# A hybrid decoder layer: the order of two token norms, the first transfers, and how x is added to three blocks of the output projection

## The chip, the cores and the metric

The kernel runs on one core of one Trainium2 chip (trn2). The metric is the device time of one execution in microseconds (us); less is better. The kernel before took 2128.58 us, the median of three runs (2126.21, 2128.58 and 2132.4).

## What is computed

One decoder layer over 512 tokens of width 2048, with 256 memory tokens. All inputs and the output are float32.

```python
xn = rms_norm(x, attn_norm_g)
gq, gk, gv, gg, ga, fq, fk, fv, fg, ff, mq, mg = split(xn @ w_in)
gla_o = gla_chunked(...)                 # 8 gated-linear-attention heads
fox_o = forgetting_attention(...)        # 4 heads
mem_o = softmax(mq . mk) @ mv            # 4 heads; mk, mv = rms_norm(mem, mem_norm_g) @ w_mem_kv
o = rms_norm(concat(gla_o, fox_o, mem_o), out_norm_g)
h = x + (o * gates) @ w_out
u = relu(rms_norm(h, mlp_norm_g) @ w_up)
y = h + (u * u) @ w_down
```

`rms_norm(v, g)` is `v * rsqrt(mean(v*v) + 1e-6) * g`.

## The kernel before, in words

**Precision.** Every operand of a large product is split in two: a rounded high part, which ScalarE writes (a CAST, L168 or L367; `ahi_x` L186 for x), and the remainder, which VectorE writes from the operand and the high part (a TENSOR_TENSOR, L169 or L367; `alo_x` L187). One product then takes three matmuls, high by high (L176), high by low (L177), low by high (L178), in `mm3`. A weight tile is thus loaded by a DMA from SyncE (SP), cast by ScalarE (ACT), subtracted by VectorE (DVE), and only then multiplied by TensorE (PE).

**Stages.** The program goes through the input projection, the attentions, the output projection (`out_pair`, twice), the up projection (eight groups) and the down projection. The input projection begins with `project("gk", "gq")`, which goes over 16 tiles of x and multiplies each by two groups of columns. After it come four products `in_pair(n, c)`, c outside and n inside. `in_pair` and `out_pair` are written as seven block products, in the order 1, 5, 6, 3, 7, 2, 4 (as in Strassen's scheme, with sums of blocks as operands); a product is two steps in an `in_pair` and four in an `out_pair`, one split weight tile (128x1024) to a step. When a product is complete, `after` empties its two PSUM banks.

**The norm of x.** The input projection multiplies x without its norm; the factor of each token, `xrstd`, is applied when banks are emptied. `x_tile(k)` loads x's tile (`xraw`), splits it and adds its squares to `xacc`. `token_rstd` (L222) then sums `xacc` over the partitions by four small matmuls (`ss_x`, L226) and computes 1/sqrt with a chain of small operations on DVE and ACT (`s_x` L119, `y_x` L120 and L121, `z_x` L122 to L124, `r_x` L125). The banks of the first product of `in_pair(0, 0)` are emptied by ACT with that factor (`o`, L492), so they wait for `r_x`.

**The memory's norm.** Before the pairs the kernel loads 16 tiles of the memory (`memT`, L509), squares them (ACT, `sq_mem`, L219), adds the squares (DVE, into a part of `spare`, L220) and calls `token_rstd` again (`ss_mem`, two small matmuls on PE at L226). The factor is first used in the memory's projections, after the pairs.

**The sums of x.** Four of the seven products of a pair have sums of blocks of x as operands. `x_sums(0)` writes those of c = 0 into `sh` and `sl`. `x_sums(1)` computes those of c = 1 and writes them to DRAM (`x_op`, by DMAs from GpSimd, POOL). While `in_pair(1, 0)` runs (n = 1, c = 0), `next_sums` brings each of the four back when the product that read its place is done: a load on SP (L450), a copy by ACT (L451), a subtraction by DVE (L452).

**The output projection.** Its first pair emits h's left half in blocks (row, column) of 256 tokens by 512 columns. `block(r, c)` loads x's block into a staging tile (L1270, SP), and the products add into it: 1 to (0,0), 5 to (1,1), 6 to (0,1), then 3, 7, 2 and 4. Each bank is added by DVE (L1275). `finish` writes a complete block to DRAM and prepares it for the up projection.

**What sets the order.** A scheduler places instructions on the engines' queues by priority and by when it estimates that operands are ready; `high_priority` moves one forward, and `issue_after` puts one behind another. Each engine works through its queue in order.

Of the kernel before, what the change touches and what calls it, by code (L numbers as in the profile page):

```python
# [9 lines left out]
F32 = mybir.dt.float32  # L10
# [8 lines left out]
NT = S // 128  # L19
# [28 lines left out]
def hybrid_layer(  # L48
# [45 lines left out]

    colt = const.tile([128, 68], F32, name="colt")
    with tc.high_priority(offset=AHEAD):
        nc.sync.dma_start(colt, cols)
    g_attn, g_mem, g_out, g_mlp = (colt[:, 16 * i : 16 * i + 16] for i in range(4))
    g_fq, g_fk, g_mq, g_mk = (colt[:, 64 + i : 65 + i] for i in range(4))

# [93 lines left out]
    def tmp(name, tag, n=512, dt=F32):  # L194
        return tp.tile([128, n], dt, tag=tag, name=name, bufs=TAGS[tag])
# [36 lines left out]
    def project(*groups):  # L232

        banks = [[(abank if i else gbank)(f"{g}_{t}") for t in range(NT)] for i, g in enumerate(groups)]
        for kp in range(NK // 2):
            for ps, group in zip(banks, groups):
                wh, wl = wtile(w_in[GROUPS.index(group), kp], f"{group}{kp}", parts=1 if kp else 2)
                for kk in range(2):
                    k = 2 * kp + kk
                    ah, al = x_tile(k)  # L240
                    for t in range(NT):
                        cs = slice(kk * 512 + t * 128, kk * 512 + t * 128 + 128)
                        mm3(ps[t], wh[:, cs], wl[:, cs], ah, al, k == 0, k == NK - 1)
        return [p for ps in banks for p in ps]
# [159 lines left out]


    kq = project("gk", "gq")
    xrstd = token_rstd(xacc, NT, "x")
    kTs = bigt(0, [128, NT, 512], "kTs")
    qTs = bigt(1, [128, NT, 512], "qTs")
    with urgent():  # L410
# [36 lines left out]

    def next_sums(n):
        hi, lo = sh[:, n, :, :], sl[n // 2][:, n % 2, :, :]
        nc.sync.dma_start(lo.bitcast(F32), x_op[n])  # L450
        A.copy(hi, lo.bitcast(F32))  # L451
        V.tensor_sub(lo, lo.bitcast(F32), hi.bitcast(F32))  # L452


    places = [[(1, 1), (1, 2)], [(0, 0), (0, 1)], [(0, 2), (1, 0)]]
# [1 line left out]
    class Pair(Weights):  # L457
# [16 lines left out]
        def left(self, p, j, u):  # L474
# [5 lines left out]
            at = u * 128 + (256 if p == 4 else 0)  # L480
            return xh[k][:, at : at + 128], xl[k][:, at : at + 128]

    def in_pair(n, c):
        def evict(p, acc):
            r, col = WHERE[p]
            for u in range(2):
                t = 2 * r + u
                dst = o[:, t, n * 1024 + col * 512 : n * 1024 + col * 512 + 512]
                if c or p in (3, 7, 2):
                    V.scalar_tensor_tensor(dst, acc[u], rs_x(t), dst, op0=ALU.mult, op1=ALU.add)  # L490
                else:
                    A.activation(dst, acc[u], AF.Copy, scale=rs_x(t))  # L492

        def after(p, acc):
            empty(evict, p, acc)
            if (c, n) == (0, 1) and p in SUMS:
                with tc.high_priority(offset=AHEAD):
                    next_sums(SUMS[p])

        multiply(Pair(n, c), after)  # L500

# [2 lines left out]

    macc = spare[:, 3072 : 3072 + M]
    with tc.issue_after(turned_kq[0].ins), tc.issue_after(turned_kq[1].ins):
        for k in range(NK):
            mt = tmp(f"memT_{k}", "ta", M)
            nc.sync.dma_start(mt, memT[k])  # L509
            add_squares(macc, mt, k == 0, f"mem{k}")  # L510
        x_sums(1)
    mrstd = token_rstd(macc, MT, "mem")
    for c in range(2):
        for n in range(2):
            in_pair(n, c)
    blocks.close()
    n_hl = 2
    turns["raw"] = 0
# [744 lines left out]
    def out_pair(n):  # L1263
# [6 lines left out]
                nc.sync.dma_start(z[r, c].rearrange("p (t n) -> p t n", t=2), x[r, 2 * n + c])  # L1270

        def evict(p, acc):
            for t in range(2):
                v = z[WHERE[p]][:, t * 512 : t * 512 + 512]
                V.tensor_add(v, v, acc[t])  # L1275

        def after(p, acc):
            r, c = WHERE[p]
# [51 lines left out]
        def inside(p, q):  # L1330
# [6 lines left out]
            if not n and q > 1 and p in (3, 7, 2):  # L1337
                for cs in ((slice(1024, 1536), slice(1536, 2048)) if q > 2 else (slice(0, 1024),)):
                    in_turn({3: S3, 7: A12, 2: A22}[p], cs)
            if q == 0 and p in (1, 6, 5, 4):  # L1340
                block(*WHERE[p])
            if q == 1:
                rest()
# [234 lines left out]
```

## Time and profile before

| | |
|---|---|
| runs | 2126.21, 2128.58, 2132.4 us |
| the profiled execution's own time | 2126.06 us |
| its span, first to last instruction | 2124.0 us |
| PE busy | 2100.5 us, 99% |
| DVE busy | 1615.4 us, 76% |
| ACT busy | 1133.3 us, 53% |
| POOL busy | 152.1 us, 7% |
| mean granted clock of PE | 0.998 of full speed |

Busy time is that of compute instructions; register, branch and DMA-issuing instructions are not in it. Matmuls overlap, so a matmul's own duration is longer than the distance from one to the next. The distance between the starts of two 128x512 matmuls is about 0.23 us at full clock (2.4 GHz) and 0.43 us at half (1.2 GHz). In a timeline a row has the start, the duration, the engine, the line, the operation, output and inputs, and in square brackets the idle time of that engine just before it with what ended it.

### The profile page before, as it was taken

The numbers are of one execution on the slowest core, as the hardware profiler recorded it, in microseconds if no ns is written. First come the engines' busy times: TensorE is split into PE (matmuls) and PEld (weight loads), VectorE is DVE, ScalarE is ACT, GpSimd is POOL, SyncE is SP. The second block draws the span as 40 slices with busy tenths as digits, with TensorE's granted clock in tenths as the row PEclk, the third lists the DMA queues.
The fourth block names the chain that finished last, engine by engine and source line by source line (L and its number), as shares of the span: only waits on it lengthen the run. The fifth ranks groups of instructions, "written<-read, shape, count | busy, mean of one in ns | idle before, by whom it ended". The sixth has DMA issues, their size and how long they took to land.

```text
span 2124.0 us, 25538 instructions
## 1 busy us (share of the span) xinstructions
PE 2100.5 (99%) x9746; PEld 1733.4 (82%) x9746; DVE 1615.4 (76%) x1747; ACT 1133.3 (53%) x1607; POOL 152.1 (7%) x220
## 2 busy tenths in 40 slices
PE   8999999999999999999999999999999999999999
PEld 7777878887788788888888888888888888888887
DVE  6579888764664899977777777778968868777875
ACT  6454364434563565755555555556646546556543
POOL 0012000000000022100000000000100000000000
PEclk9999999999999999999999999999999999999999
DMA  7355342121224666353353353355677668668653
GB/s 264 97 164 168 118 139 93 60 70 60 85 91 143 237 256 216 112 208 120 131 206 119 130 207 119 129 208 199 207 208 236 176 196 254 168 187 268 182 174 129
DMA packets 78755, 347.09 MB, mean 163 GB/s; under 512 B 9305, under 2 KB 13401, under 8 KB 57130
## 3 DMA queue, kind: packets, MB, share of 16 engines
q1 hardware_dynamic: 58778, 274.95, 37.1%
q0 software_dynamic: 19856, 70.53, 12.5%
q8 instruction: 76, 1.25, 0.2%
q14 instruction: 45, 0.37, 0.1%
HBM read 271.52 MB, written 73.92 MB: 163 GB/s over the span
## 4 chain that ended last, share of the span: by engine, by line
PE 95%; DVE 2%; DMA 1%; ACT 1%; issue 1%; SPq 0%; DVEq 0%; ACTq 0%
PE acc_up L177 9%; PE acc_up L178 9%; PE acc_up L176 9%; PE acc_dn L178 9%; PE acc_dn L177 9%; PE acc_dn L176 9%; PE acc_in L177 2%; PE acc_in L176 2%; PE acc_in L178 2%; PE acc_out L177 2%; PE acc_out L178 2%; PE acc_out L176 2%; PE gg L176 1%; PE gg L178 1%; PE gg L177 1%; PE ut L1394 1%
## 5 line engine op out<-in xcount | busy, mean ns | idle before, releaser
L367 DVE TENSOR_TENSOR hl_up<-raw_up,hl_up 128x1024 fp32r<-128x1024 f32 x224 | 273.0, 1223 | 141.0 <-ACT hl_up L367 139.6
L367 DVE TENSOR_TENSOR hl_dn<-raw_dn,hl_dn 128x1024 fp32r<-128x1024 f32 x224 | 272.8, 1222 | 125.0 <-ACT hl_dn L367 124.7
L367 ACT CAST hl_up<-raw_up 128x1024 fp32r<-128x1024 f32 x224 | 235.0, 1050 | 204.4 <-PE acc_up L178 136.0
L367 ACT CAST hl_dn<-raw_dn 128x1024 fp32r<-128x1024 f32 x224 | 234.7, 1053 | 195.5 <-PE acc_dn L178 146.5
L315 DVE TENSOR_TENSOR raw_dn<-raw_dn,raw_dn 128x2048 f32<-128x2048 f32 x64 | 146.3, 2286 | 0.4
L315 DVE TENSOR_TENSOR raw_up<-raw_up,raw_up 128x2048 f32<-128x2048 f32 (+1 forms) x62 | 140.6, 2267 | 0.0
L367 ACT CAST hl_out<-raw_out 128x1024 fp32r<-128x1024 f32 x56 | 58.0, 1050 | 48.8 <-PE acc_out L178 21.4
L1492 ACT COPY m<-acc_dn 128x512 f32<-128x512 f32 x96 | 55.7, 587 | 43.0 <-PE acc_dn L178 42.9
L1493 POOL DMA_DIRECT2D hd<-m x48 | 41.5, 865 | 515.5 <-ACT m L1492 515.5
L367 DVE TENSOR_TENSOR hl_out<-raw_out,hl_out 128x1024 fp32r<-128x1024 f32 x56 | 72.5, 1306 | 6.6 <-ACT hl_out L367 6.2
L367 ACT CAST hl_hl_in<-spare 128x1024 fp32r<-128x1024 f32 x31 | 32.3, 1050 | 51.3 <-DVE spare L472 30.0
L1386 POOL DMA_DIRECT2D op<-u x32 | 17.1, 535 | 559.5 <-ACT u L1395 554.6
L1409 ACT ACTIVATE z<-z,rstd 128x512 f32<-128x512 f32 x48 | 32.2, 716 | 44.9 <-DVE z L1458 44.9
L176 PE MATMUL acc_in<-hl_hl_in,sh 128*128 128x512 f32 x128 | 50.9, 400 | 2.8 <-ACT o L492 2.8
L176 PE MATMUL gg<-ahi_x,hl_gg 128*128 128x512 f32 x128 | 53.5, 418 | 0.0
L177 PE MATMUL acc_in<-hl_hl_in,sh 128*128 128x512 f32 x128 | 51.1, 399 | 0.0
L178 PE MATMUL acc_in<-hl_hl_in,sl 128*128 128x512 f32 x128 | 50.8, 397 | 0.0
L176 PE MATMUL acc_up<-hl_up,left0h 128*128 128x512 f32 x128 | 50.5, 394 | 0.0
L176 PE MATMUL acc_up<-hl_up,left5h 128*128 128x512 f32 x128 | 50.5, 394 | 0.0
L176 PE MATMUL acc_up<-hl_up,left1h 128*128 128x512 f32 x128 | 50.5, 394 | 0.0
L176 PE MATMUL acc_up<-hl_up,left2h 128*128 128x512 f32 x128 | 50.5, 394 | 0.0
L177 PE MATMUL acc_dn<-hl_dn,left 128*128 128x512 f32 x128 | 50.0, 391 | 0.4 <-DVE hl_dn L367 0.3
(542 smaller groups left out, 6245.2 us busy)
## 6 DMA issues: line engine op xcount, KB each, us to landing
raw_up<-in_w_up_dram SPq DMA_DIRECT2D x64, 1024.0 KB, 6.2
raw_dn<-in_w_down_dram SPq DMA_DIRECT2D x64, 1024.0 KB, 6.9
hd<-m POOLq DMA_DIRECT2D x48, 512.0 KB, 6.5
raw_out<-in_w_out_dram SPq DMA_DIRECT2D x16, 1024.0 KB, 5.8
op<-u POOLq DMA_DIRECT2D x32, 512.0 KB, 4.2
op<-s POOLq DMA_DIRECT2D x24, 512.0 KB, 3.1
spare<-in_w_pair_dram SPq DMA_DIRECT2D x16, 512.0 KB, 4.7
raw_in<-in_w_pair_dram SPq DMA_DIRECT2D x16, 512.0 KB, 4.1
```

Of the source, the lines that this page charges most:

```text
L176: T.matmul(ps, lhsT=ah, rhs=bh, start=start, stop=False, skip_group_check=on)
L177: T.matmul(ps, lhsT=ah, rhs=bl, start=False, stop=False, skip_group_check=on)
L178: T.matmul(ps, lhsT=al, rhs=bh, start=False, stop=stop, skip_group_check=on)
L315: V.tensor_sub(dst, a, b)
L367: turns["made"] = made = A.copy(hi, part), V.tensor_sub(lo, part, hi.bitcast(F32))
L1386: nc.gpsimd.dma_start(down_op[c][i][:, half * 1024 : half * 1024 + 1024], tile)
L1394: T.transpose(tps[:, m * 128 : m * 128 + 128], z[:, t * 512 + m * 128 : t * 512 + m * 128 + 128], ident)
L1409: A.activation(dst, src, AF.Relu, scale=rstd[:, 2 * row + t : 2 * row + t + 1])
L1492: A.copy(st[:, t * 512 : t * 512 + 512], acc[t])
L1493: nc.gpsimd.dma_start(dst, st.rearrange("p (t n) -> p t n", t=2), accum_op=ALU.add)
```

## The change

It has four parts.

1. The table of the norms' gains, `colt`, is loaded by POOL's queue instead of SP's, and `project` calls `x_tile` ahead of the weight tile of each step.
2. `token_rstd` of x runs at a raised priority.
3. The memory's loads, squares and additions stand behind `in_pair(0, 0)`, and the memory's `token_rstd` behind all four pairs. In `next_sums` the load is issued after a product as before, while the copy and the subtraction are called after the product that follows.
4. In the first output pair products 1, 5 and 6 are copied from PSUM by ACT into a staging tile, and x is added to that tile by an accumulating DMA from POOL. The three loads of x's blocks and the six additions of DVE for them go away; block (1,0), product 4, stays as it was.

```diff
-        nc.sync.dma_start(colt, cols)
+        nc.gpsimd.dma_start(colt, cols)
...
             for ps, group in zip(banks, groups):
+                x_tile(2 * kp)
                 wh, wl = wtile(w_in[GROUPS.index(group), kp], f"{group}{kp}", parts=1 if kp else 2)
...
-    xrstd = token_rstd(xacc, NT, "x")
+    with urgent():
+        xrstd = token_rstd(xacc, NT, "x")
...
-        nc.sync.dma_start(lo.bitcast(F32), x_op[n])
-        A.copy(hi, lo.bitcast(F32))
-        V.tensor_sub(lo, lo.bitcast(F32), hi.bitcast(F32))
+        with tc.high_priority(offset=AHEAD):
+            nc.sync.dma_start(lo.bitcast(F32), x_op[n])
+
+        def landed():
+            A.copy(hi, lo.bitcast(F32))
+            V.tensor_sub(lo, lo.bitcast(F32), hi.bitcast(F32))
+
+        return landed
...
+    waiting_sums = []
...
         def after(p, acc):
             empty(evict, p, acc)
+            if waiting_sums:
+                waiting_sums.pop()()
             if (c, n) == (0, 1) and p in SUMS:
-                with tc.high_priority(offset=AHEAD):
-                    next_sums(SUMS[p])
+                waiting_sums.append(next_sums(SUMS[p]))
...
-        for k in range(NK):
-            mt = tmp(f"memT_{k}", "ta", M)
-            nc.sync.dma_start(mt, memT[k])
-            add_squares(macc, mt, k == 0, f"mem{k}")
         x_sums(1)
-    mrstd = token_rstd(macc, MT, "mem")
     for c in range(2):
         for n in range(2):
             in_pair(n, c)
+            if not c and not n:
+                for k in range(NK):
+                    mt = tmp(f"memT_{k}", "ta", M)
+                    nc.sync.dma_start(mt, memT[k])
+                    add_squares(macc, mt, k == 0, f"mem{k}")
+    mrstd = token_rstd(macc, MT, "mem")
...
         def evict(p, acc):
+            r, c = WHERE[p]
+            added = not n and p in (1, 5, 6)
+            if added:
+                z[r, c] = stage(f"x_{n}_{r}{c}")
             for t in range(2):
-                v = z[WHERE[p]][:, t * 512 : t * 512 + 512]
-                V.tensor_add(v, v, acc[t])
+                v = z[r, c][:, t * 512 : t * 512 + 512]
+                if added:
+                    A.copy(v, acc[t])
+                else:
+                    V.tensor_add(v, v, acc[t])
+            if added:
+                nc.gpsimd.dma_start(z[r, c].rearrange("p (t n) -> p t n", t=2), x[r, 2 * n + c], accum_op=ALU.add)
...
-            if q == 0 and p in (1, 6, 5, 4):
+            if q == 0 and p in ((1, 6, 5, 4) if n else (4,)):
                 block(*WHERE[p])
```

How the instructions stand now, at three places.

The first is ACT's queue at the very start, where `hl_gk` is the first weight tile of `gk` (in two halves), `ahi_x` the high part of an x tile, and `xacc` the first tile's squares. Before:

```order
L168 CAST hl_gk_116<-raw_gk_115 128x512
L186 ACTIVATE ahi_x_125<-xraw_123,colt 128x512
L216 ACTIVATE xacc<-xraw_123 128x512
L168 CAST hl_gk_116<-raw_gk_115 128x512
L186 ACTIVATE ahi_x_144<-xraw_142,colt 128x512
```

With the change:

```order
L186 ACTIVATE ahi_x_117<-xraw_115,colt 128x512
L216 ACTIVATE xacc<-xraw_115 128x512
L168 CAST hl_gk_123<-raw_gk_122 128x512 x2
L186 ACTIVATE ahi_x_144<-xraw_142,colt 128x512
```

Both casts of the first weight tile now stand behind the first x tile's two operations.

The second is DVE's queue at the end of the first projection, where the norm of x is computed; `hl_hl_in` are low parts of the weight tiles of `in_pair(0, 0)`, L472 (now L479) forms sums of weight blocks, and L220 adds memory squares. Before:

```order
L119 TENSOR_SCALAR s_x<-ss_x 128x4
L367 TENSOR_TENSOR hl_hl_in_51_1041<-spare,hl_hl_in_51_1041 128x1024
L472 TENSOR_TENSOR raw_in_010_1020<-raw_in_110_1058,raw_in_010_1020 128x1024
L122 TENSOR_TENSOR z_x<-y_x 128x4
L367 TENSOR_TENSOR hl_hl_in_60_1062<-spare,hl_hl_in_60_1062 128x1024
L472 TENSOR_TENSOR spare<-spare 128x1024
L123 TENSOR_TENSOR z_x<-z_x,s_x 128x4
L220 TENSOR_TENSOR spare<-spare,sq_mem_831 128x256
L124 TENSOR_SCALAR z_x<-z_x 128x4
L220 TENSOR_TENSOR spare<-spare,sq_mem_836 128x256
L125 TENSOR_TENSOR r_x<-y_x,z_x 128x4
```

With the change:

```order
L119 TENSOR_SCALAR s_x<-ss_x 128x4
L122 TENSOR_TENSOR z_x<-y_x 128x4
L123 TENSOR_TENSOR z_x<-z_x,s_x 128x4
L124 TENSOR_SCALAR z_x<-z_x 128x4
L125 TENSOR_TENSOR r_x<-y_x,z_x 128x4
L368 TENSOR_TENSOR hl_hl_in_51_949<-spare,hl_hl_in_51_949 128x1024
L479 TENSOR_TENSOR raw_in_010_928<-raw_in_110_966,raw_in_010_928 128x1024
```

The five small operations of the norm now stand together, ahead of the weight tiles' work, and no memory square is among them.

The third is ACT's queue at the entry of the output projection's product 6; `acc_out_1_..` and `acc_out_5_..` are the banks of products 1 and 5, and `hl_out_60` to `hl_out_63` the four weight tiles of product 6. Before:

```order
L367 CAST hl_out_53_5966<-raw_out_001_5744 128x1024
L1128 CAST left3h<-scores 128x512
L367 CAST hl_out_60_5986<-raw_out_000_5742 128x1024
L367 CAST hl_out_61_5990<-raw_out_000_5742 128x1024
```

With the change:

```order
L368 CAST hl_out_53_5964<-raw_out_001_5744 128x1024
L1139 CAST left3h<-scores 128x512
L1291 COPY x_00_5959<-acc_out_1_0_5853 128x512
L1291 COPY x_00_5959<-acc_out_1_1_5854 128x512
L1291 COPY x_11_6003<-acc_out_5_0_5891 128x512
L1291 COPY x_11_6003<-acc_out_5_1_5892 128x512
L368 CAST hl_out_60_5984<-raw_out_000_5742 128x1024
L368 CAST hl_out_61_5988<-raw_out_000_5742 128x1024
```

Four copies out of PSUM, two of them of product 5's banks, now stand between `left3h` and the first cast of product 6.

## Rows read from the trace of the kernel before

**Rows 1.** The page: busy time of each engine, its share of the span, and instructions.

```profile
PE 2100.5 (99%) x9746; PEld 1733.4 (82%) x9746; DVE 1615.4 (76%) x1747; ACT 1133.3 (53%) x1607; POOL 152.1 (7%) x220
```

**Rows 2.** The waits of PE over the whole run, by what was waited for: total us, times, longest us.

```profile
PE gk L176 <- ACT ahi_x L186: 6.0, 1, 6.0
PE ss_mem L226 <- DVE spare L220: 3.4, 1, 3.4
PE acc_in L177 <- DVE hl_hl_in L367: 2.8, 2, 1.8
PE acc_in L176 <- ACT o L492: 2.8, 1, 2.8
PE acc_out L177 <- DVE hl_out L367: 1.9, 4, 0.6
```

**Rows 3.** The timeline of PE from 105 to 122 us: the first matmul after product 1 of `in_pair(0, 0)` with the wait before it, and the stretch around the memory's sums.

```profile
105.70 0.50 PE L176 MATMUL acc_in<-hl_hl_in,sh 128*128 128x512 f32 x1 [2.76 <-ACT o L492]
...
111.05 0.39 PE L178 MATMUL acc_in<-hl_hl_in,sl 128*128 128x512 f32 x1
114.82 0.90 PE L226 MATMUL ss_mem<-wide,spare 128*128 128x1 f32 x4 [3.38 <-DVE spare L220]
115.59 0.77 PE L176 MATMUL acc_in<-hl_hl_in,sh 128*128 128x512 f32 x1
...
121.96 0.40 PE L176 MATMUL acc_in<-hl_hl_in,sh 128*128 128x512 f32 x1
```

**Rows 4.** The timeline of DVE in the same place: the first and the last operation of the norm of x (nine others lie between them).

```profile
97.39 0.16 DVE L119 TENSOR_SCALAR s_x<-ss_x 128x4 f32<-128x4 f32 x1 [1.61 <-PE ss_x L226]
...
104.49 0.15 DVE L125 TENSOR_TENSOR r_x<-y_x,z_x 128x4 f32<-128x4 f32 x1
```

**Rows 5.** The chain of waits: the two transfers in it that stand ahead of the memory's sums and of the sums of x. Start, us, what.

```profile
111.14 2.05 DMA memT<-in_memT_dram
170.54 3.36 DMA sl<-x_op
173.93 1.06 ACT sh L451
```

**Rows 6.** Busy time of the engines in stretches: from:to, length, then PE, PEld, DVE, ACT and POOL (busy us and instructions), the granted clock, the DMA engines' share and GB/s.

```profile
92.00:184.00 92.00, 83.77 (x358) 67.86 (x356) 72.97 (x98) 53.54 (x79) 20.95 (x41) 0.96 0.53 171
97.00:126.00 29.00, 22.86 (x89) 18.18 (x89) 16.25 (x36) 17.09 (x36) 2.35 (x4) 0.88 0.46 136
745.00:750.00 5.00, 5.00 (x24) 4.14 (x23) 5.00 (x6) 0.33 (x1) 0.00 (x0) 1.00 0.00 0
755.00:760.00 5.00, 4.74 (x23) 3.75 (x24) 4.94 (x5) 3.05 (x5) 0.54 (x1) 1.00 0.63 216
```

**Rows 7.** Groups of DVE's instructions from 92 to 184 us: busy us and mean ns, then the idle time before them with its releasers.

```profile
L367 DVE TENSOR_TENSOR hl_hl_in<-spare,hl_hl_in 128x1024 fp32r<-128x1024 f32 x13 | 16.0, 1230 | 6.5 <-ACT hl_hl_in L367 6.5
L367 DVE TENSOR_TENSOR hl_hl_in<-raw_in,hl_hl_in 128x1024 fp32r<-128x1024 f32 x13 | 15.7, 1223 | 3.7 <-ACT hl_hl_in L367 3.6
```

**Rows 8.** The chain of waits in the first microseconds: start, us, what.

```profile
0.81 0.39 SPq L97
1.72 3.39 DMA xraw<-in_xT_dram
```

**Rows 9.** The timeline of POOL, ACT and PE there.

```profile
0.80 0.20 POOL masks.py:197 MEMSET ident<- 128x128 f32 x1 [0.29 <-POOLq L1568]
...
5.19 0.72 ACT L186 ACTIVATE ahi_x<-xraw,colt 128x512 fp32r<-128x512 f32 x1 [0.48 <-DMA xraw<-in_xT_dram]
5.82 0.61 ACT L216 ACTIVATE xacc<-xraw 128x512 f32<-128x512 f32 x1
...
7.77 0.63 PE L176 MATMUL gk<-ahi_x,hl_gk 128*128 128x512 f32 x1
```

**Rows 10.** From issue to landing, the transfers of tile `x_op`: sixteen stores of 128 KB on POOL's queue and four loads on SP's, in one row.

```profile
DMA to landing us min/median/max: 2.0/3.8/6.6
```

**Rows 11.** The same of the transfers of tile `hd`: 48 of 512 KB from POOL that accumulate (L1493), and 16 others, in one row.

```profile
DMA to landing us min/median/max: 2.9/5.5/9.8
```

**Rows 12.** The entry of the output projection's product 6, and its product 7 (the last two rows): timelines of ACT, DVE and PE.

```profile
728.34 1.06 ACT L367 CAST hl_out<-raw_out 128x1024 fp32r<-128x1024 f32 x1 [2.91 <-DVE raw_out L359]
...
729.96 1.22 DVE L367 TENSOR_TENSOR hl_out<-raw_out,hl_out 128x1024 fp32r<-128x1024 f32 x1
...
729.03 0.39 PE L178 MATMUL acc_out<-hl_out,left3l 128*128 128x512 f32 x1
...
731.24 0.50 PE L177 MATMUL acc_out<-hl_out,left 128*128 128x512 f32 x1 [0.63 <-DVE hl_out L367]
...
734.78 0.50 PE L177 MATMUL acc_out<-hl_out,left 128*128 128x512 f32 x1 [0.51 <-DVE hl_out L367]
...
754.82 0.50 PE L177 MATMUL acc_out<-hl_out,left5h 128*128 128x512 f32 x1 [0.48 <-DVE hl_out L367]
...
758.75 0.50 PE L177 MATMUL acc_out<-hl_out,left5h 128*128 128x512 f32 x1 [0.26 <-DVE hl_out L367]
```

**Rows 13.** The timeline of DVE in product 7: the last addition to block (0,1) and the sum of weight blocks behind it.

```profile
754.68 0.68 DVE L1275 TENSOR_TENSOR x<-x,acc_out 128x512 f32<-128x512 f32 x1
755.27 2.29 DVE L315 TENSOR_TENSOR raw_out<-raw_out,raw_out 128x2048 f32<-128x2048 f32 x1
```

**Rows 14.** A group of the page: ACT's copy of a PSUM bank (busy us, mean ns).

```profile
L1492 ACT COPY m<-acc_dn 128x512 f32<-128x512 f32 x96 | 55.7, 587 | 43.0 <-PE acc_dn L178 42.9
```

## The prediction

> **What bounds the kernel now.** I read the page's busy times first: PE is busy for 99% of the span, DVE for 76% [rows 1]. So time is gained only where PE stands idle or runs at half clock, and I next read PE's waits over the whole run [rows 2]. Five lines hold nearly all of them: 6.0 us before the first matmul, 3.4 us for the memory's squares, 2.8 us in two waits for weight tiles of the pairs, 2.8 us for an emptied bank, and 1.9 us in four waits for weight tiles of the output projection. Each part of the change aims at one of the five; what it gives is at most that wait, less what takes its place.
>
> The timeline of PE shows the second and the fourth of them in one place, at 102 to 122 us [rows 3]. The first wait, 2.76 us, ends when ACT has emptied a bank with the norm of x; the second, 3.38 us, when DVE has added the last memory square. Behind the second the matmuls run at 0.43 us apart and not at 0.23: from 115.59 to 121.96 fifteen start, 6.37 us where full clock would take 15 x 0.227 = 3.40. The windows give a granted clock of 0.88 for 97 to 126 us [rows 6]. So the gap of 3.38 us, or the 2.76 us just before it together with it, also cost 2.97 us of half clock (1.2 GHz); the 2.76 us alone was followed by matmuls at full pitch (2.4 GHz).
>
> Why r_x was late stands on DVE: its chain began at 97.39 and ended at 104.49, though the five operations are of 0.16 us each [rows 4]; they stood between weight tiles of 1.23 us [rows 7] and memory squares. Why the squares were late stands in the chain of waits: the last transfer of `memT` landed at 113.2 [rows 5].
>
> **The change part by part.** The sum is made against the profiled execution's own 2126.06 us.
>
> *Start.* Without `colt` ahead of it, and with x asked for before the weights, x's first transfer is issued at 0.81 and not 1.72; with the same 3.39 us it lands at 4.20 [rows 8]. ACT then does `ahi_x` (0.63 apart), `xacc` (0.52) and both casts. From x's landing (5.11) to the first matmul's start was 0.86 us with the cast done already; now it is about 1.8 (both ACT operations and a cast stand before it), and the fourth matmul, which the second tile half gates, comes about 3.1 us after landing: 4.20 + 3.09 = 7.29 against 7.77 [rows 9]. Gain 0.5. `colt` is now POOL's; POOL is free at 0.80 [rows 9], and the only rows for small transfers of that queue, those of `x_op`, say 2.0 to 6.6 us with a median of 3.8 [rows 10], so that it lands at 2.8 to 7.4, at the median 4.6. At the median x and `colt` come nearly together and 0.1 is left of the gain; at the late end the start loses 2.7 (7.4 + 3.09 = 10.49); if x comes faster than the 3.39 by half a microsecond it gains 1.0. I take 0.5, since `x_op`'s rows are of a busy stretch of four times the bytes (128 KB against 34).
>
> The Trainium skill, "DMA: Bandwidth & Descriptors", section "Latency and other measured facts", puts the first byte at about 1 us for GpSimd's queue against about 0.6 us for SyncE's. By that `colt` would come 0.4 us later than on SP and x alone would decide, an estimate of 0.5 us gained; no row here shows such a first byte.
>
> *The norm of x.* `ss_x` goes to PE five matmuls earlier, and the chain stands together on DVE. From `s_x` at 97.39 [rows 4], five DVE operations and two of ACT of some 0.2 us each make `r_x` ready near 98.7. Product 1's last matmul starts at 102.56 (105.70 less the 2.76 and one matmul's length [rows 3]), and PE now does product 5 next, which needs no emptied bank, 24 x 0.227 = 5.4 us. So the bank is emptied in time by several us: -2.8. I allow +0.1 for `ss_x`, which waits for one bank of `gq`. The weight tile that the chain passes is held up for 0.8 us, within what the pairs' buffers hold.
>
> *The memory's squares.* The 16 loads, squares and additions go behind the first pair's instructions, into the stretch of the second, and the two small matmuls behind the fourth, over 60 us later. The wait goes: -3.4. They took 0.77 us to the next start (114.82 to 115.59) at half clock; at full clock I take half of that: -0.4. And the 2.97 us of half clock has no gap left to follow: -3.0. That the squares take DVE and ACT time elsewhere costs nothing so long as DVE has room there; see the first rival.
>
> *The sums of x.* In the chain the load `sl<-x_op` took 3.36 us from 170.54, ACT's copy began only at 173.93 [rows 5], and ACT's next casts and then DVE's splits were behind it; the two waits of the pairs, 2.8 us together [rows 2], follow. With the copy and subtraction a product later (5.4 us of PE) the load has landed before ACT comes to it: -2.8, with 0 as the other end.
>
> *Output projection.* Before, ACT cast the first tile of product 6 at 728.34 and DVE subtracted it at 729.96, once its two additions were through; PE waited until 731.24 [rows 12]. Now four copies stand in front of that cast on ACT. The last of them waits for the last matmul of product 5 (729.03 + 0.39) and takes 0.59 [rows 14], so the cast comes at 730.05, the subtraction at 731.15, PE at 732.45: 1.2 late, and at the second tile still 1.1 (735.85 for 734.78). DVE in return loses six additions of 0.6 us, so the two waits in product 7, 0.48 and 0.26 [rows 12], go: -0.7. Together +0.4; -1.4 if DVE's room also removes the waits of product 6 and +3 if the gap there costs half clock too.
>
> The three accumulating transfers themselves are used late, except block (0,1). Its copies end at about 745.7 (product 6 ends near 742.8 and two casts of `left` stand between the copies; an estimate from ACT's order). The DMA engines idle from 745 to 750 [rows 6]; issue 0.9 and the 5.5 us median of the rows nearest to it, those of `hd` [rows 11], put the landing at 752 to 753, and DVE's addition, which needs it, stood at 754.68 [rows 13]. So it costs nothing by 2 us, and it is late by 2 us at the 9.8 us end. The removed loads of x were issued 20 us ahead and held nobody: nothing.
>
> The sum: -0.5 - 2.8 + 0.1 - 3.4 - 0.4 - 3.0 - 2.8 + 0.4 = **-12.4**, from 2126.06 to 2113.7. The median of the runs shown lies 2.5 above that execution and the fastest at its level; I add 0.8 and forecast **2114.5**.
>
> **The rivals.**
>
> *A. DVE becomes the bound of the pairs.* It worked 73.0 of the 92 us from 92 to 184 [rows 6]. Take out PE's idle and half-clock time there (12.4) and the same work stands in 79.6 us: 92%. DVE itself waited 10.2 us for casts in that stretch [rows 7]; if all of that stays, it needs 83.2 us and returns 3.6. The memory's squares wait for loads that ACT stands in line for, 2.05 us each [rows 5]; two such waits that reach PE give the same size. For it: the pairs have few buffers. Against: PE lets casts go a few steps ahead, and 48 us of the pairs (126 to 174) went without a wait. Time: 2118.
>
> *B. The entry of product 6 costs a clock drop.* The waits there, 1.2 + 0.6 us and then about 1.0, come near the 3.38 us that was followed by half clock; the 2.76 us alone was not. Price 3.0 as there. Time: 2117.5.
>
> *C. `colt` is late on POOL.* Price 3.2 against the forecast (2.7 lost where 0.5 was counted). Time: 2117.5.
>
> *D, slower than before.* POOL can't get its transfers out while DVE works. DVE is busy for 5.00 of 5 us at 745 to 750 [rows 6], so the three accumulating transfers would pile up in POOL's queue, in order, with that of block (0,1) last. DVE works in order too: it would stop at its addition to block (0,1), which stood at 754.68 [rows 13], and hold every weight tile behind it, and PE. Only then would the three go out, 0.9 us apart; the last lands 5.5 us later by the median and 9.8 by the longest row of `hd` [rows 11], between 762.8 and 767.2. With 3.0 us of half clock after the stop it costs 11.1 to 15.5, so 2125.6 to 2130; from a landing at about 766 on, the kernel is slower than before. Against: from 755 to 760 POOL issued a transfer in 0.54 us while DVE was busy for 4.94 of 5 us [rows 6].
>
> The Trainium skill, "SBUF — State Buffer", in the box on the "DVE blocks DMA" trap, states that rule: while VectorE runs an operation in a two-port mode, GpSimd is locked out and cannot write its descriptors. The row from 755 to 760 disagrees for the operations that DVE runs here.
>
> That the change does nothing where it means to would need the scheduler to put the squares back; the order of the changed kernel shows they are not.
>
> **How the numbers follow.** About 0.3% (6.4 us of the median) is what a measurement can tell from no change, so faster means below 2122.2 and slower above 2135. The forecast itself has 0.62; A 0.13, B 0.06 and C 0.04 all stay below 2122 and make it 0.85 for faster. D has 0.04, all of it in between, as its longest landing gives 2130. The last 0.11 is for waits that only the new order makes and no row shows, 0.08 of it in between and 0.03 above. So faster 0.85, same 0.12, slower 0.03. The low end takes the start at -1.0, the seam at -1.4 and no offset to the median (2113.7 - 0.5 - 1.8 = 2111.4), and a little for a wait that goes with the rest: 2110.5. The high end takes A and B together (3.6 + 3.0): 2121.
>
> **What would show it.** In the changed profile PE's waits should have no line for `ss_mem` and none for `acc_in` from ACT's `o`; the granted clock from 97 to 126 us should be 1.00; the two `acc_in` L177 waits should be gone; the first `acc_out` L177 wait should have grown to some 2 us, with a copy of L1291 ahead on ACT; and the first matmul should start near 6.0 with the fourth near 7.3. It is wrong if PE waits for `hl_hl_in` in the pairs (A), if matmuls run 0.43 us apart after product 5 of the output projection (B), if ACT's first `ahi_x` waits for `colt` (C), or if DVE's addition in product 7 waits for a transfer (D).

## The result, and the profile after

The changed kernel took 2118.48 us, the median of four runs (2117.22 to 2120.03), against 2129.55 for four of the kernel before: a ratio of 0.9949, 95% interval 0.9932 to 0.9966, about 11 us. Measured a second time it gave 2115.74 us and 0.9942 (0.9930 to 0.9953). The profiled execution took 2120.03 us with a span of 2118.3, only 6.0 less than the profile of before; the experiments show why that pair of profiles understates it.

PE's waits over the whole run after the change, as in [rows 2] (what was waited for: total us, times, longest us):

```profile
PE gk L176 <- ACT hl_gk L168: 7.8, 1, 7.8
PE acc_dn L177 <- DVE hl_dn L368: 2.0, 5, 0.7
PE acc_out L176 <- ACT hl_out L368: 1.6, 1, 1.6
PE acc_in L177 <- DVE hl_hl_in L368: 1.0, 2, 0.8
...
PE acc_out L177 <- DVE hl_out L368: 0.5, 1, 0.5
```

The lines for `ss_mem` and for ACT's `o` are gone, and of the pairs' waits 1.0 of 2.8 us is left. The first matmul comes later, not earlier (7.8 for 6.0), and product 6 of the output projection has a wait of 1.6 us that it did not have.

The windows of [rows 6]:

```profile
92.00:184.00 92.00, 91.72 (x408) 75.23 (x407) 82.60 (x106) 59.02 (x83) 23.37 (x41) 1.00 0.52 175
97.00:126.00 29.00, 29.00 (x132) 24.07 (x131) 22.64 (x35) 19.88 (x29) 7.00 (x13) 1.00 0.60 190
```

PE is busy for 29.00 of 29 us at a granted clock of 1.00 where it had 22.86 at 0.88; DVE works 82.6 of 92 us (90%).

Where the gain lies is read best from the starts of matmuls that mark a stage, taken from PE's timelines. The table has the difference to the first profile of before; each column after the first is what one stretch added (the four sums leave out 0.5 us or less elsewhere). The marks are the first matmul of `in_pair(0, 0)`, the first behind the four pairs that is not one of the memory's two small ones, the first of either output pair, and the first of the down projection with the last matmul of all.

| kernel | up to the first pair | the pairs | output projection, first pair | down projection |
|---|---|---|---|---|
| before, profiled again | -0.76 | +2.25 | +0.05 | +2.74 |
| changed | +1.36 | -10.92 | +0.53 | +3.54 |
| changed, profiled again | -0.07 | -11.90 | +0.53 | +1.90 |
| squares in front | +1.23 | -2.02 | -0.09 | +2.76 |
| norm not urgent | +0.62 | -10.89 | +0.56 | +2.01 |
| sums at once | -0.43 | -8.09 | +0.54 | +0.62 |
| output projection of before | +0.31 | -11.22 | +0.03 | -0.49 |
| table behind x | -0.64 | -11.03 | +0.54 | -0.05 |
| only squares | -1.55 | -9.34 | +0.03 | +2.77 |
| both mends | -0.58 | -9.69 | -1.45 | -0.74 |
| start of before, copies late | -1.32 | -9.80 | -1.47 | +1.92 |
| squares added on GpSimd | -1.07 | -6.90 | -1.46 | +3.73 |

### The profile page after: what moved, and what is told of

Same layout as the page of the kernel before. It is cut to its first block, busy times and chain, and to the rows that moved or that the text cites. A ratio compares the mean times of both kernels' runs of the same rounds, so it can differ in the third digit from the quotient of the medians.

```text
span 2118.3 us, 25535 instructions
## 1 busy us (share of the span) xinstructions
PE 2099.2 (99%) x9746; PEld 1732.2 (82%) x9746; DVE 1611.0 (76%) x1741; ACT 1135.7 (54%) x1613; POOL 156.0 (7%) x224
## 4 chain that ended last, share of the span: by engine, by line
PE 95%; DMA 2%; DVE 2%; ACT 1%; issue 0%; SPq 0%; ACTq 0%; DVEq 0%; POOLq 0%
PE acc_up L177 10%; PE acc_up L178 10%; PE acc_up L176 9%; PE acc_dn L177 9%; PE acc_dn L178 9%; PE acc_dn L176 9%; PE acc_out L177 2%; PE acc_out L178 2%; PE acc_out L176 2%; PE acc_in L177 2%; PE acc_in L178 2%; PE acc_in L176 2%; PE gg L176 1%; PE gg L178 1%; PE gg L177 1%; PE ut L1414 1%
## 5 line engine op out<-in xcount | busy, mean ns | idle before, releaser
L177 PE MATMUL acc_dn<-hl_dn,left3h 128*128 128x512 f32 x128 | 50.4, 394 | 0.8 <-DVE hl_dn L368 0.7
L177 PE MATMUL acc_in<-hl_hl_in,sh 128*128 128x512 f32 x128 | 50.3, 393 | 0.9 <-DVE hl_hl_in L368 0.8
L177 PE MATMUL acc_up<-hl_up,left 128*128 128x512 f32 x128 | 50.1, 391 | 0.2 <-DVE hl_up L368 0.2
```

Source lines behind the costliest of these rows:

```text
L177: T.matmul(ps, lhsT=ah, rhs=bl, start=False, stop=False, skip_group_check=on)
```

## The experiments

**1. The changed kernel again.** No edit.

> The changed kernel once more, profiled again. In its first profile 3.5 us of the gain were given back in the down projection, whose order the change does not touch (five waits for hl_dn, 2.0 us, where before had one of 0.3). Theory (that is scatter between executions): these waits come out differently this time, by more than 1 us in sum. Rival (it is the change's doing): about 2.0 us of them again, at the same tiles, near 1820, 1829, 1832, 1983 and 1986 us.

2115.74 us. The waits for `hl_dn` came out as 1.4 us in three (2.0 in five before):

```profile
PE acc_dn L177 <- DVE hl_dn L368: 1.4, 3, 0.8
```

That is 0.6 less and not the more than 1 us that the theory asked for, so this run alone leaves it open. The other profiles settle it: their waits for `hl_dn` run from 0 to 2.2 us and the table's last column from -0.74 to +3.73, with the order there the same in all, and the kernel before itself has +2.74 the second time (experiment 11). The first profile of before has one of the least disturbed down projections of the thirteen; the 3.5 us "given back" in the changed kernel's first profile are scatter between executions and not the change's doing.

**2. The memory's squares in front again.**

```diff
-            if not c and not n:  ...  # squares behind in_pair(0, 0)
+        for k in range(NK):  ...      # squares ahead of x_sums(1) and the pairs, token_rstd(macc) too
```

> The changed kernel with the memory's loads, squares and two small matmuls ahead of the pairs, as before; the norm of x stays urgent. Theory (the wait and its half clock are the squares' own): TensorE waits 3 to 4 us for ss_mem again and runs some 15 matmuls at half clock; 6 to 7 us more than the changed kernel. Rival (the squares were late only because the norm of x and they were interleaved): a wait under 1.5 us, no half clock, 1 us or less more.

2126.81 us, ratio 0.9995 (0.9987 to 1.0003): nearly all of the gain is gone, 8.3 to 11.1 us by the two medians of the changed kernel, more than the theory's 6 to 7 us. The rival's short wait did not come. PE's timeline says why:

```profile
109.55 0.40 PE L178 MATMUL acc_in<-hl_hl_in,sl 128*128 128x512 f32 x1
116.08 0.98 PE L226 MATMUL ss_mem<-wide,spare 128*128 128x1 f32 x4 [6.14 <-DVE spare L220]
116.93 0.77 PE L176 MATMUL acc_in<-hl_hl_in,sh 128*128 128x512 f32 x1
117.50 0.63 PE L177 MATMUL acc_in<-hl_hl_in,sh 128*128 128x512 f32 x1
```

The norm of x is urgent here and PE waits for it no more. But the wait for the squares has grown from 3.38 to 6.14, by just the 2.76 that went [rows 3]: PE arrived earlier at a thing that was no earlier. The two waits stood in series in front of one end, the last of the memory's 16 tiles. Behind the wait eleven matmuls run at half clock, from 117.50 on.

**3. Only the squares moved**, in the kernel before.

```diff
-        for k in range(NK):  ...      # squares ahead of x_sums(1)
+            if not c and not n:  ...  # squares behind in_pair(0, 0); token_rstd(macc) behind all pairs
```

> The kernel before with one edit: the memory's loads, squares and two matmuls moved as in the change. Theory (both waits at 102 to 115 us and the half clock hang on the squares; the run with the squares in front had one wait of 6.14 us in place of 2.76 and 3.38): no ss_mem wait, no wait for the bank, 9.2 us less up to the second pair; with the sums' waits staying (2.8), 2119 us; if they go too, 2116 us. Rival (the norm's priority is worth its 2.8 us by itself): a wait of 2 to 2.8 us for the bank stays, 2122 us.

2117.74 us, 0.9955 (0.9943 to 0.9967), an interval that overlaps both of the changed kernel's: in time, the squares' move alone can't be told from the whole change. The pairs take 9.34 us less (expected 9.2), and the wait for the bank that the rival asked for is not there. Here the norm's chain is as spread out as before:

```profile
95.83 0.16 DVE L119 TENSOR_SCALAR s_x<-ss_x 128x4 f32<-128x4 f32 x1 [1.61 <-PE ss_x L226]
102.89 0.15 DVE L125 TENSOR_TENSOR r_x<-y_x,z_x 128x4 f32<-128x4 f32 x1
```

It takes 7.1 us, as in [rows 4], and PE does not wait for it: with the squares away the scheduler puts product 5 ahead of 6, and product 5 needs no emptied bank. The weight tiles' waits stay, as the theory had it (one of the four, 0.7 us at 143, stands ahead of the sums' place):

```profile
PE acc_in L177 <- DVE hl_hl_in L367: 2.7, 4, 0.9
```

**4. The norm not urgent**, the rest as changed.

```diff
-    with urgent():
-        xrstd = token_rstd(xacc, NT, "x")
+    xrstd = token_rstd(xacc, NT, "x")
```

> The changed kernel without the raised priority of x's norm; the squares stay behind the first pair. In its order TensorE does product 5 ahead of 6 all the same. Theory (product 5's 5.4 us cover the norm's chain even where weight tiles stand between its steps, since r_x came 2 us after product 1's end before): no wait for ScalarE's emptying of the bank, time the same as the changed kernel's. Rival (the priority is what removed the wait): 1 to 2.8 us of wait for it ahead of product 6, time as much more.

2117.65 us, 0.9954 (0.9942 to 0.9966), overlapping the changed kernel's two; no wait for the bank; the pairs take 10.89 us less, within the spread of the changed kernel's 10.92 and 11.90. The last step of the norm's chain began 5.7 us later than in the changed kernel (whose row is the second), and PE did not wait for it:

```profile
105.06 0.15 DVE L125 TENSOR_TENSOR r_x<-y_x,z_x 128x4 f32<-128x4 f32 x1
...
99.39 0.16 DVE L125 TENSOR_TENSOR r_x<-y_x,z_x 128x4 f32<-128x4 f32 x1
```

By the pairs, the priority is worth between 0 and 1 us beside the squares' move, not 2.8.

**5. The sums' copy at once.**

```diff
-        def landed():
-            A.copy(hi, lo.bitcast(F32))
-            V.tensor_sub(lo, lo.bitcast(F32), hi.bitcast(F32))
-        return landed
+        A.copy(hi, lo.bitcast(F32))
+        V.tensor_sub(lo, lo.bitcast(F32), hi.bitcast(F32))
...
-            if waiting_sums:
-                waiting_sums.pop()()
...
```

> The changed kernel with the sums' copy and subtraction called right behind their load again, as before. Theory (ScalarE stood waiting for the load, so the deferral is what removed the two waits): waits for hl_hl_in of 1 to 3 us in sum come back around 165 to 180 us, time 2.8 us above the changed kernel's. Rival (the loads were late because the stores of the sums were, behind the memory's squares): waits under 0.5 us more than in the changed kernel, time the same.

2118.12 us, 0.9955 (0.9943 to 0.9967): by the ratios 1.3 to 2.8 us more than the changed kernel, with intervals that overlap. The pairs take 8.09 us less than before's: 2.8 to 3.8 us of the changed kernel's gain is missing. Waits for weight tiles came back, though 1.7 of the 3.4 us stand at 133 us, ahead of the sums' place, where kernels with the deferral have up to 1.7 us too (experiment 9):

```profile
PE acc_in L177 <- DVE hl_hl_in L368: 2.5, 3, 0.9
...
PE acc_in L176 <- ACT hl_hl_in L368: 0.9, 1, 0.9
```

So the stage does not give the deferral's price cleanly. PE's waits in the sums' place, from 160 to 195 us, do it better. They are 2.8 and 4.4 us in the two profiles of before; 1.7 here and 2.0 in experiment 3, where the squares are moved and the copies are not deferred; nothing in experiment 2, where the copies are deferred and the squares are not moved; and 0 to 1.2 in the eight profiles with both. So the deferral alone removes them, the squares' move alone takes a part of them, and behind the squares' move the deferral is worth some 2 us.

The reason that the theory gives did not show. ACT waits for the sums' loads about as long in before, in the changed kernel and here (in this order, from 150 to 190 us):

```profile
ACT sh L451 <- DMA sl<-x_op: 3.6, 2, 3.1
ACT sh L456 <- DMA sl<-x_op: 3.2, 3, 1.7
ACT sh L453 <- DMA sl<-x_op: 3.3, 2, 2.2
```

What the deferral changed is DVE's order. In the changed kernel (the first two rows) the sum of weight blocks goes ahead of the sums' subtraction, here behind it:

```profile
169.24 1.21 DVE L479 TENSOR_TENSOR raw_in<-spare,raw_in 128x1024 f32<-128x1024 f32 x1
170.38 1.25 DVE L457 TENSOR_TENSOR sl<-sl,sh 128x1024 fp32r<-128x1024 f32 x1
...
169.03 1.21 DVE L454 TENSOR_TENSOR sl<-sl,sh 128x1024 fp32r<-128x1024 f32 x1
170.16 1.25 DVE L474 TENSOR_TENSOR raw_in<-spare,raw_in 128x1024 f32<-128x1024 f32 x1
```

ACT's cast of that weight tile thus came at 171.53 instead of 170.56, the low part at 172.61 instead of 171.65, and PE waited 0.77 us for it at 173.89.

The rival's cause was there as well. In before, SyncE's queue stood waiting for the stores of the sums, the last of which POOL sent at 165 us; in the changed kernel and here they went out by 128, and no such wait is left:

```profile
SPq L450 <- DMA x_op<-st: 6.3, 2, 5.7
```

**6. The output projection of before.**

```diff
-                if added:
-                    A.copy(v, acc[t])
-                else:
-                    V.tensor_add(v, v, acc[t])
-            if added:
-                nc.gpsimd.dma_start(..., accum_op=ALU.add)
+                V.tensor_add(v, v, acc[t])
...
-            if q == 0 and p in ((1, 6, 5, 4) if n else (4,)):
+            if q == 0 and p in (1, 6, 5, 4):
```

> The changed kernel with the output projection of before (three loads of x, six additions on VectorE). Theory (the fourth part costs 0.5 us: 1.6 + 0.5 of waits at product 6's first tile for 0.2 + 0.6 + 0.5, and 0.7 in product 7 less): the wait for ScalarE's cast at product 6 goes, four waits of 0.2 to 0.7 for VectorE's low parts come back; time 0.5 us less than the changed kernel's, which is inside the scatter. Rival (the accumulating transfers disturb later transfers, up to the down projection, 3.5 us): time 3 to 4 us less, with the waits of the down projection gone.

2116.92 us, 0.9941 (0.9929 to 0.9953). In time it can't be told from the changed kernel; by stage the output projection takes 0.50 us less. So the fourth part costs half a microsecond in the five profiles in which half clock follows its wait (+0.53 to +0.56). The rival is out: the kernel of experiment 7 has the same accumulating transfers, and its down projection is at -0.05. The way the fourth part costs it is in PE's timeline of the changed kernel:

```profile
721.46 0.73 PE L176 MATMUL acc_out<-hl_out,left 128*128 128x512 f32 x2 [1.62 <-ACT hl_out L368]
722.72 0.50 PE L177 MATMUL acc_out<-hl_out,left 128*128 128x512 f32 x1 [0.53 <-DVE hl_out L368]
723.05 0.48 PE L178 MATMUL acc_out<-hl_out,left 128*128 128x512 f32 x1
723.32 0.63 PE L176 MATMUL acc_out<-hl_out,left 128*128 128x512 f32 x1
...
726.31 0.55 PE L178 MATMUL acc_out<-hl_out,left 128*128 128x512 f32 x1
726.70 0.39 PE L176 MATMUL acc_out<-hl_out,left 128*128 128x512 f32 x1
```

Eight matmuls run at half clock from 723.32 to 726.70 (3.38 us where 8 x 0.227 = 1.82), which in turn covers the wait at the second tile. In experiment 2 the same waits (1.62 and 0.53) were followed by full clock; there PE waited 0.7 us at the second tile, and that output projection came out at -0.09. In product 7 neither kernel has a wait: those went with DVE's additions.

**7. The table behind x.** The cause at the start:

```profile
1.36 0.69 POOL L97 DMA_DIRECT2D colt<-in_cols_dram  x1 [0.85 <-POOLq L1588]
...
6.03 0.72 ACT L186 ACTIVATE ahi_x<-xraw,colt 128x512 fp32r<-128x512 f32 x1 [3.95 <-DMA colt<-in_cols_dram]
```

In the changed kernel's timeline ACT waits for `colt`, which POOL issued at 1.36 and which landed at 6.01, 4.65 us later. The edit:

```diff
-        nc.gpsimd.dma_start(colt, cols)
+        nc.sync.dma_start(x_first, xT[0])
+        nc.sync.dma_start(colt, cols)
...
```

> The changed kernel with the gains' table back on SyncE's queue, issued right behind the first x tile. Theory (the table was late because GpSimd's queue sent it at 1.36 us and it took 4.65 us): it is issued near 1.25 and lands near 3.1 to 4; x lands near 4.2 and ScalarE starts then; first matmul near 6.0 instead of 7.84, gq's first matmul 1.0 to 1.5 us earlier than 15.94, the time 1 to 1.5 us less than the changed kernel's. Rival (the first microseconds' transfers hold each other up, so x itself lands near 6): first matmul still after 7, time unchanged.

2115.43 us, 0.9939 (0.9926 to 0.9952), an interval that overlaps the changed kernel's two: the mend shows at the start and not in the time. The first matmul is at 5.92, and ACT no longer waits for the table:

```profile
3.58 0.63 ACT L219 ACTIVATE xacc<-xraw 128x512 f32<-128x512 f32 x1 [1.50 <-DMA xraw<-in_xT_dram]
4.12 0.70 ACT L188 ACTIVATE ahi_x<-xraw,colt 128x512 fp32r<-128x512 f32 x1
5.25 0.62 ACT L170 CAST hl_gk<-raw_gk 128x512 fp32r<-128x512 f32 x1 [0.42 <-DMA raw_gk<-in_w_in_dram]
5.92 0.79 PE L178 MATMUL gk<-ahi_x,hl_gk 128*128 128x512 f32 x1 [5.92 <-ACT hl_gk L170]
```

gq's first matmul came at 13.96, 2.0 us before that of the profile after and 0.6 before that of its repeat. The rival is out: ACT began on x at 3.58. What ACT waits for last is now the first weight tile, which is asked for behind x and the table and was there at 5.2. In before x was asked for last and landed at 5.1. The first matmul needs both, so that it comes at 5.92 here and at 5.97 there.

**8. Both mends**: the table as in 7, and product 5's copies behind product 6's casts.

```diff
         seam.append(made[1])
+        seam.append(made[0])
...
                         es.enter_context(tc.issue_after(seam[1].ins))
+                        es.enter_context(tc.issue_after(seam[2].ins))
```

> The changed kernel with two mends: the gains' table on SyncE's queue behind the first x tile, and ScalarE's copies of product 5's two banks behind the casts of product 6's weight tiles instead of ahead of them. Theory: first matmul near 5.9; TensorE's wait of 1.62 us for ScalarE's cast at product 6 goes and the low part's 0.5 stays; 1.5 us less than with the table's mend alone, 2 to 2.5 us less than the changed kernel, 2113.5 us. Rival (the copies in their late place hold casts of product 3 or the accumulating transfers): a wait of as much at product 3, nothing gained over the table's mend.

2112.93 us, 0.9929 (0.9917 to 0.9941): with the next one the fastest kernel here. The wait for ACT's cast at product 6 is gone, no matmul there runs at half clock, and the output projection takes 1.98 us less than in the changed kernel (-1.45 for +0.53). Of the output projection's waits only those for low parts at the first two tiles of product 6 are left, none at product 3, so the rival is out:

```profile
PE acc_out L179 <- DVE hl_out L371: 1.2, 2, 0.7
```

The ratio's interval overlaps the changed kernel's; the stage's times do not.

**9. The start of before with the late copies.**

```diff
-                x_tile(2 * kp)
...
-        nc.gpsimd.dma_start(colt, cols)
+        nc.sync.dma_start(colt, cols)
...
```

(The two `seam` lines are those of experiment 8.)

> The changed kernel with its first part undone (table ahead of x on SyncE, weights asked for before x, as before) and product 5's copies behind the casts. Theory (the first part gains nothing even with the table's mend, since the kernel with only the squares moved began gq at 13.24 and the mended one at 13.96): first matmul near 6, time within 0.5 us of the kernel with both mends. Rival (x first is worth its 0.5 us once the table is not late): 0.5 us or more slower than it.

2112.75 us, 0.9936 (0.9924 to 0.9949), the same as both mends; its first matmul is at 5.82 and theirs at 5.83. The first part gains nothing even when mended.

**10. The squares' additions on GpSimd**, on top of both mends.

```diff
-            V.tensor_add(acc, acc, sq)
+            eng.tensor_tensor(acc, acc, sq, op=ALU.add)   # eng=G for the memory
```

> The kernel with both mends (table on SyncE behind x, product 5's copies behind the casts), and the fifteen additions of the memory's squares on GpSimd instead of VectorE. Theory (VectorE, busy for 90% of 92 to 184 us, is what is left to wait for in the pairs): it is busy for 6 us less there, the waits for hl_hl_in, 1 to 2 us in sum, fall under 0.5, time 0.5 to 1.5 us less than with both mends. Rival (these waits come from ScalarE, which stands in line for transfers of the memory): waits as before, time the same.

2117.53 us, 0.9955 (0.9942 to 0.9967), slower than with both mends: its pairs took 2.8 us more, and the waits there grew:

```profile
PE acc_in L179 <- DVE hl_hl_in L371: 2.6, 4, 1.2
...
PE acc_in L178 <- ACT hl_hl_in L371: 1.1, 1, 1.1
```

Both expectations failed: it is not the same and not better. ACT's waits from 120 to 160 us show what was late:

```profile
ACT sq_mem L222 <- DMA memT<-in_memT_dram: 6.5, 7, 2.1
ACT rows_r L556 <- POOL spare L223: 4.1, 1, 4.1
```

An addition of 128x256 takes GpSimd 1250 ns (423 on VectorE with both mends). ACT comes to a wait for the last one, 4.1 us until 150.18 (1.7 with both mends); two casts stand behind it, at 150.72 and 151.65, and PE waits 1.06 and 0.76 us for them at 151.79 and 153.06, with seven matmuls at half clock behind. PE's longest wait, 1.2 us at 144.57, has another source: its cast waited until 142.92 for DVE's sum of weight blocks.

So the added waits came through ACT and through DVE. With both mends, ACT's line reaches PE in one place, at 132 to 134 us (waits of 0.4 and 0.8 us), where two casts stand behind loads of the memory's tiles:

```profile
131.19 0.42 ACT L222 ACTIVATE sq_mem<-memT 128x256 f32<-128x256 f32 x1 [1.44 <-DMA memT<-in_memT_dram]
131.51 1.03 ACT L371 CAST hl_hl_in<-spare 128x1024 fp32r<-128x1024 f32 x1
...
132.59 0.50 PE L178 MATMUL acc_in<-hl_hl_in,ahi_x 128*128 128x512 f32 x1 [0.42 <-ACT hl_hl_in L371]
```

What the other waits there come from (0.2 to 0.4 us at 167, 173 and 228 us) is open, and so is DVE's part in them.

**11. Before again.**

> The kernel before once more, with a profile. Theory (the down projection's waits are scatter, and its first profile had few): the waits in the pairs and at the squares as in the first profile within 0.5 us, those of the down projection another sum, anywhere from 0 to 2 us, and the time of this profile 1 to 4 us above 2126.06. Rival (before is free of them): 0.3 us again.

2127.61 us, 0.9995 (0.9986 to 1.0004); its profiled execution took 2130.41, 4.35 above the first, a little more than the theory's 1 to 4. The down projection's waits came out at 1.6 us, as the theory allowed, and the rival is out. The pairs were not within 0.5 us, as it asked, but 2.25 us slower than in the first profile: 1.65 us in the waits for weight tiles (three for two), 0.24 in the wait for the squares, and some 0.4 in half clock, which now stood behind the first wait too and was shorter behind the second:

```profile
104.95 0.50 PE L176 MATMUL acc_in<-hl_hl_in,sh 128*128 128x512 f32 x1 [2.77 <-ACT o L492]
...
106.00 0.52 PE L177 MATMUL acc_in<-hl_hl_in,sh 128*128 128x512 f32 x1
106.32 0.63 PE L178 MATMUL acc_in<-hl_hl_in,sl 128*128 128x512 f32 x1
106.75 0.63 PE L176 MATMUL acc_in<-hl_hl_in,sh 128*128 128x512 f32 x1
```

## Why the prediction was right, and where it was not

The forecast of 2114.5 us lies 1.2 to 4.0 below the two medians, inside its range. That is in part luck: the start missed by more than 1 us, and the output projection came near its figure by a way that was not in the sum. Step by step:

*The pairs (-12.3 in sum) held.* They gave 10.9 and 11.9 against the first profile of before, and 2.25 more against its second. The wait for the squares, the half clock behind it and the wait for the bank all went, and most of the rest is the 0.6 to 1.0 us of waits that stayed.

*The split among them failed in one step.* I gave the norm's priority 2.8 and the squares 6.8. Experiment 2 has the priority without the squares moved, and the pairs gain 2.0 in all, no more than the sums' part; experiments 3 and 4 have the squares moved without the priority, and the wait goes. I had seen that PE would do product 5 ahead of 6, and still booked the wait under the norm: what removed it was that order, which came with the squares' move (in experiment 2 product 6 still stands ahead of 5).

*The sums (-2.8)* are about right in size and wrong in the way. With the copy a product later the load was to have landed before ACT comes to it; but ACT still waits 3.2 us for these loads (3.6 before). The deferral, worth some 2 us behind the squares' move, works through DVE's order. And the squares' move, which I did not count here, had a part: with it the stores of the sums no longer came late (experiment 5).

*The start (-0.5) failed, in sign.* `colt`'s landing on POOL was bounded by 2.8 to 7.4 us, and I took x as the later of the two, since `x_op`'s transfers have four times the bytes. It landed at 6.01: issued at 1.36 and not at 0.80, and then 4.65 us under way, longer than the 3.8 us median of the larger ones [rows 10]. Rival C, with 0.04, happened; its price was 3.2, and by gq's first matmul it cost 1.6 and 0.2 (15.94 and 14.53, for 14.3 by the forecast, which is the 14.80 of before less 0.5). In six executions with the table on POOL, ACT could start between 4.55 and 6.03, and gq's first matmul came at 15.1 on the mean; in four with the start of before, at 13.8. That first profile of before, from which I reckoned, has the latest start of the four. I also took x as the only load that gates the start: experiment 7 shows that the weight tile, asked for behind x, then comes last and takes the gain. The Trainium skill, "DMA: Bandwidth & Descriptors", section "Latency and other measured facts", has about 1 us to the first byte for GpSimd's queue and about 0.6 us for SyncE's; with the 1.8 us that the table took on SyncE's queue in before, that makes 2.2 us, an estimate. The trace disagrees: from issue to landing it took 3.2 to 4.7 us in the six executions.

*The output projection (+0.4)* measured +0.53, and not quite by the way I gave. With the copies ahead of the cast PE waited 1.6 + 0.5 us at the first tile, and its second matmul there came 1.1 us later than before (1.2 by the forecast); the waits of product 7 went. But rival B, the clock drop, happened as well, in five of the six profiled executions with the copies in this place: at 0.6 us net and not 3.0, since PE, slowed, no longer ran ahead of the second tile. Without the drop the stage came out at -0.09, not +0.4, so that the near hit is luck.

*Block (0,1) was in time, so D did not happen.* The accumulating transfers landed after 7.3 us (median of three; I took 5.5):

```profile
x<-in_x_dram POOLq DMA_DIRECT2D x3, 512.0 KB, 7.3
...
736.64 0.85 POOL L1295 DMA_DIRECT2D x<-in_x_dram  x1 [14.65 <-ACT x L1291]
...
745.21 1.44 DVE L1293 TENSOR_TENSOR x<-x,acc_out 128x512 f32<-128x512 f32 x2
```

That of block (0,1) itself took 5.3 us, from 736.64 to 741.90. DVE's additions to this block, those of product 3, began at 745.21 without a wait, 3.3 us after the landing (2 by the forecast). POOL issued the transfer in 0.85 us while DVE was busy for 0.81 of 0.9. The Trainium skill, "SBUF — State Buffer", in the box on the "DVE blocks DMA" trap, speaks of operations that DVE runs in a two-port mode. DVE's operations there are TENSOR_TENSORs, and no run here shows whether they run in such a mode: the row does not put that rule to the test, and the "disagrees" of the prediction said too much.

*Rival A* came in small: DVE's 90% was foreseen as 92%, and 0.6 to 1.0 us of waits stayed (3.6 at most). The one at 133 us stands behind ACT's line for the memory's loads, as A had it (the rows are in experiment 10); whether DVE bounds the others is open.

## What to carry to other kernels

Two waits of one engine that lead to the same late end are one wait: taking the first away lengthened the second here (3.38 grew by 2.76 to 6.14), and only what ends last is worth moving. A small load that gates the first instruction belongs on the queue that is known to be quick; whether it stood ahead of x or behind it made no difference to the first matmul, which needs x and a weight tile and waits for whichever is asked for last. Copies that nobody needs soon must be put behind the casts that the bound engine waits for, since a priority alone doesn't know who is waiting. When a wait of the bound engine goes, look whether the wait that was to be its cause went too: ACT's did not, and the gain came by DVE. A single profile is no measure of a few microseconds: look up, by stage, whether the stages that the change does not touch moved as well.

## What the runs showed of the hardware that I had not expected

A gap of one size is not always followed by half clock: 2.76 us was not in one execution of the kernel before and 2.77 was in another; 1.62 + 0.53 us at product 6 was in five executions and not in a sixth. At the start, when full clock was granted varied more than the first matmul did. In the eight profiles whose first matmul came between 5.7 and 6.4 us, the matmuls ran at half clock until 9.6 at the earliest (experiment 3) and 12.47 at the latest (the first profile of before), and gq's first matmul came between 13.24 and 14.80. So a difference of a microsecond at that mark, in one profile, is not the order's doing by itself.
